# Weight splits and the residual around a LayerNorm boundary: a new order in a two-layer hybrid decoder step

## The chip, the cores and the metric

The kernel runs on one core of a Trainium2 chip. The metric is the device time of one execution in microseconds (us); a lower time is better. Times of before and after are compared on the same chip. TensorE is called PE below, VectorE DVE, ScalarE ACT, GpSimd POOL, and SyncE, which issues most loads, SP.

## The reference

One inference step for a prompt of 256 tokens and for 8 samples of 4 tokens, with shared weights: 288 columns in all. Layer 0 mixes tokens with gated linear attention (GLA), layer 1 with dilated window attention over one shared K/V. Each layer is feed-forward, mixer, feed-forward, and each sub-layer ends in a LayerNorm whose input is the scaled residual plus the gated result. Shift, scale and gate (adaLN) come from nine modulations per layer, `silu(c) @ w_ada`.

```
def post_norm(x, y, gate, g, b):
    return layer_norm(ALPHA * x + (1.0 + gate[:, None, :]) * y, g, b)

# per layer l, with sh, sc, g from silu(c) @ w_ada[l]
y = swiglu(modulate(x, sh1, sc1), w_ffn1_up[l], w_ffn1_down[l])
x = post_norm(x, 0.5 * y, g1, ln_g[l, 0], ln_b[l, 0])
h = modulate(x, sh2, sc2)
y = gla_mixer(h, ...) if l == 0 else dilated_mixer(h, ...)
x = post_norm(x, y, g2, ln_g[l, 1], ln_b[l, 1])
y = swiglu(modulate(x, sh3, sc3), w_ffn2_up[l], w_ffn2_down[l])
x = post_norm(x, 0.5 * y, g3, ln_g[l, 2], ln_b[l, 2])
```

Before layer 1 the shared K/V are projected from a modulated x. D_MODEL is 1024, D_FF 2816, all data float32.

## The kernel before

Activations lie transposed: 8 chunks of 128 features by 288 columns. A float32 product is made of three matmuls in a faster format: each operand is split into a high half and the low rest, and high x high, high x low and low x high are added in PSUM (`mm3`, lines 531 to 533).

**Weights** come through `Stream`: one list of jobs in the order of use, each cut into pieces of 512 KB. A piece is loaded by SP into one of 11 raw buffers as soon as the piece 11 places ahead of it has been released (`pump`). A piece of a projection weight is called a part. `split_part` makes its high half on ACT (line 177) and its low half on DVE (line 179), into one of 4 pairs of buffers. `take` hands out a job's halves and splits the next job's parts; `more(n)` splits n further parts ahead of time. adaLN weights are not split: they are multiplied as they are (line 450), and `fill` handles those at the head of the list. `weave` spreads adaLN jobs between the projection weights of a stage: the first `lead` weights come alone, then the others with adaLN jobs between them.

**Order.** A scheduler orders the instructions of each engine when the program is built. `pin(chain, ins)` ties an instruction behind the one pinned before it on the same chain, so pinned instructions keep the order in which the code issues them. What is not pinned may be moved far ahead, into any pause that the scheduler sees.

**A boundary** is the end of one sub-layer and the start of the next; there are five that go through `post_norm`: (0,0) after the first feed-forward, into the GLA; (0,1) after the GLA; (0,2) after the second feed-forward, into the shared K/V; (1,0) into the dilated attention's query projections (the q stage); (1,1) after it. `Post.stats` sums squares on PE, `spread` gives the inverse deviation to all partitions (line 651). Then `scaled` makes each of the 8 chunks: DVE lines 758, 763 and 764, ACT lines 760 and 765 (the high half), DVE 767 and 769 (the low half); from the fourth chunk on DVE line 668 subtracts the mean first. All these are pinned. The chunks enter `project_chunkwise` as they come: four products side by side, 12 matmuls a chunk.

Three weight parts of the next stage are split before the boundary (`more(3)`). The fourth is split behind the third chunk, by `S.more(1)` in `post_norm`. `post_norm` also returns the generator `Post.residual`: for each chunk, line 676 on DVE and line 678 on POOL write the scaled residual into `ax`, two chunks per step. In the feed-forward stages one step is run for each of the second to fifth pair of up weights. In the GLA all of it is run behind the query projection and the gates, in the q stage behind the first four products. Line 676 is not pinned.

In the q stage `rotate` (lines 1294 to 1298, on ACT, DVE and POOL) takes each product out of PSUM, and 12 query weights are woven with eight adaLN jobs, the first four weights alone. Loads of the key and value cache follow.

Of the kernel before, what the change touches and what calls it, by code (L numbers as in the profile page):

```python
# [114 lines left out]
class Stream:  # L115
# [45 lines left out]
    def part(self, low="dve"):  # L161

        x = self.parts[self.np]
        if x >= self.nd:
            return None
        self.np += 1
        i = self.pieces[x][0]
        self.split_part(self.split.setdefault(i, Weight()), self.jobs[i], self.raw.pop(x), f"{x}", low)
        self.freed.add(x)
        self.release()  # L170
        return True

    def split_part(self, w, j, src, name, low="dve"):
        cols, nk = j["nc"], src.shape[1]
        hv, lo = [self.pool.tile([P, 1024], F32R, name=q + name, tag=q, bufs=SPLIT_BUFS)[:, 0:nk * cols]
                  .rearrange("p (k c) -> p k c", c=cols) for q in ("hi", "lo")]
        self.pin("act", self.nc.scalar.activation(hv, src, AF.Copy))  # L177
        eng = self.nc.vector if low == "dve" else self.nc.gpsimd
        self.pin(low, eng.tensor_tensor(out=lo, in0=src, in1=hv.bitcast(F32), op=ALU.subtract))  # L179
        w.append([y.rearrange("p k (m c) -> p m k c", c=min(P, cols)) for y in (hv, lo)])  # L180

    def aside(self, t, j):

# [7 lines left out]
        while self.np < len(self.parts) and self.pieces[self.parts[self.np]][0] <= i and self.part():  # L191
            pass

    def more(self, n, low="dve"):

        self.pump()
        while n and self.np < len(self.parts) and self.part(low):
            n -= 1

    def fill(self, limit=None):  # L200

# [49 lines left out]
def job_list(I):  # L251
    def ada(l, mod):
        for i in range(4):
            yield dict(kind="ada", key=("ada", l, mod, i), src=ada_src(I, l, mod, i), nk=2, nc=D)

    def adas(*which):
        return [j for l, m in which for j in ada(l, m)]

    def ffn(l, n):
        up, dn = I[f"w_ffn{n}_up"][l], I[f"w_ffn{n}_down"][l]  # L260
        out = []
        for i in range(FC // 2):
            out.append(weight_job(("a", l, n, i), up, 256 * i, 256))
            out.append(weight_job(("u", l, n, i), up, FF + 256 * i, 256))
        for cb in range(4):
            for q, (k0, nk) in enumerate(((0, 8), (8, 8), (16, 6))):
                out.append(weight_job(("d", l, n, cb, q), dn, 256 * cb, 256, k0, nk))
        return out

    win = I["w_in_a"][0]  # L270
    gla = [weight_job(("wq", i), win, 256 * i, 256) for i in range(2)]
    gla += [weight_job(("glr",), win, 2048, 16)]
    gla += [weight_job(("wk", i), win, 512 + 256 * i, 256) for i in range(2)]
    gla += [weight_job(("wv", i), win, 1024 + 256 * i, 256) for i in range(4)]
    wr = [weight_job(("wr", i), win, 2064 + 256 * i, 256) for i in range(4)]
    st = []
    for i in range(4):
        src = I["state_gla"][0, 2 * i:2 * i + 2].rearrange("b h p v -> p (b h) v")
        st.append(dict(kind="r", key=("s0", i), src=src, nk=8, nc=DV))
    wo = [weight_job(("wo", i), I["w_out_a"][0], 256 * i, 256) for i in range(4)]  # L280
    kv = [weight_job(("kv", i), I["w_kv"], 256 * i, 256) for i in range(8)]
    wq = [weight_job(("q", hq, g), I["w_q_b"][0], 1024 * g + 256 * hq, 256) for hq in range(4) for g in range(3)]
    ca = []
    steps = [(g, tp) for g in (1, 2) for tp in range(2)]
    for x in range(2 * NB + 5):
        g, tp = steps[x % 4]
        k = [cache_job(I, "cache_k", g, 2 * (x // 4) + bp, tp, ("K", g, x // 4, tp, bp)) for bp in range(2) if x < 2 * NB]
        g, tp = steps[(x - 5) % 4]
        v = [cache_job(I, "cache_v", g, 2 * ((x - 5) // 4) + bp, tp, ("V", g, (x - 5) // 4, tp, bp)) for bp in range(2) if x >= 5]
        ca += k + v  # L290
    wob = [weight_job(("wob", i), I["w_out_b"][0], 256 * i, 256) for i in range(4)]
    jobs = []
    for j in range(4):
        for h in range(2):
            src = I["w_ada"][0, 4 * h * P:4 * h * P + 4 * P, 0:2 * D].rearrange("(k p) (m c) -> p k m c", p=P, m=2)
            jobs.append(dict(kind="first", key=("first", j, h), src=src[:, :, :, 256 * j:256 * j + 256], nk=4, nc=512))
    x = GAP
    jobs += weave(ffn(0, 1)[2:], adas((0, 2), (0, 3), (0, 4)), lead=2, span=28) + adas((0, 5))[2:] + adas((0, 6))[:x]
    jobs += weave(gla + wr[:2], adas((0, 6))[x:] + adas((0, 7)), lead=5) + [st[0], st[1], wr[2], st[2], st[3], wr[3]] + wo + adas((0, 8))[1:] + adas((1, 0))[:x]
    jobs += weave(ffn(0, 2), adas((1, 0))[x:] + adas((1, 1), (2, 0), (2, 1)), lead=4, span=30)  # L300
    jobs += adas((1, 2))[2:] + adas((1, 3))[:x] + kv
    jobs += weave(ffn(1, 1), adas((1, 3))[x:] + adas((1, 4)), lead=4, span=30) + adas((1, 5))[2:] + adas((1, 6))[:x]
    jobs += weave(wq, adas((1, 6))[x:] + adas((1, 7)), lead=4) + ca + wob + adas((1, 8))[2:]
    jobs += ffn(1, 2)
    return jobs

# [13 lines left out]
def body(tc, I, O, C, dbg=None):  # L320
# [236 lines left out]
    class Post:  # L557
# [112 lines left out]
        def residual(self, l, s, rstd):  # L670
            ga = self.tile("lnga", n=DC)
            bb_ = self.tile("lnba", n=DC)
            V.tensor_scalar(out=ga, in0=lng(l, s), scalar1=ALPHA, scalar2=None, op0=ALU.mult)
            V.tensor_scalar(out=bb_, in0=lnb(l, s), scalar1=ALPHA, scalar2=None, op0=ALU.mult)
            for c in range(DC):
                V.scalar_tensor_tensor(out=ax[:, c, :], in0=z[:, c, :], scalar=ga[:, c:c + 1], in1=rstd, op0=ALU.mult,  # L676
                                       op1=ALU.mult)
                G.tensor_scalar(out=ax[:, c, :], in0=ax[:, c, :], scalar1=bb_[:, c:c + 1], scalar2=None, op0=ALU.add)  # L678
                if c % 2:
                    yield  # L680
# [90 lines left out]
    def post_norm(post, l, s, nxt):  # L771
# [4 lines left out]
        S.fill()  # L776
        rstd = post.tile("lnacc")
        last, rs = None, None
        for c in range(DC):
            if c > 2:  # L780
                post.center(c)
# [5 lines left out]
                next(last, None)  # L787
            last = step
            if c == 2:
                S.more(1)  # L790
        next(last, None)

        def rest():
# [12 lines left out]
    def first_group(xh, xl):  # L806
# [39 lines left out]
        scales(0)  # L846
        for k0 in (0, 4):
            for i in range(2):
                S.split_part(w[i], jfirst[i], wfirst[i][:, k0:k0 + 4, :], f"f{i}{k0}")
            if k0 == 0:  # L850
                fold_in(0)
        for j in range(4):
# [86 lines left out]
    def gla(xh, xl, residual):  # L939
# [75 lines left out]
        qk("wq", qT, DK ** -0.5)  # L1015
        for t in range(3):
            gates(t)
        for _ in residual:
            pass
        qk("wk", kT, 1.0)  # L1020
        b = flat("bcum")
        for t in range(2):
# [135 lines left out]

        for i in range(4):
            w_ = S.take(("wv", i))  # L1160
            for m in range(2):
                p_ = bankA()
                project(p_, w_, m, xh, xl)
# [596 lines left out]
```

## Time and profile before

| | us |
|---|---|
| median of 3 runs | 1561.36 |
| lowest, highest | 1559.15, 1568.56 |
| the profiled execution, its own time | 1566.59 |
| its span in the trace | 1564.5 |

The profiled execution lies 5.2 us above the median. Its busy shares are PE 95%, DVE 59%, ACT 46%, POOL 14%. The granted clock of PE is 0.98 on average. In the rows of the profile L676 is line 676 of the kernel, "x8" is the number of instructions in a row, and brackets give the idle time of the engine just before it and what ended it. Matmuls overlap, so the distance between two starts says more than a duration. In a table of stretches the columns are the stretch, its length, the busy time of PE, PEld (weight loads), DVE, ACT and POOL with the number of instructions, the granted PE clock, the share of DMA and GB/s.

### The profile page before, as it was taken

The numbers are of one execution on the slowest core, as the hardware profiler recorded it, in microseconds if no ns is written. First come the engines' busy times: TensorE is split into PE (matmuls) and PEld (weight loads), VectorE is DVE, ScalarE is ACT, GpSimd is POOL, SyncE is SP. The second block draws the span as 40 slices with busy tenths as digits, with TensorE's granted clock in tenths as the row PEclk, the third lists the DMA queues.
The fourth block names the chain that finished last, engine by engine and source line by source line (L and its number), as shares of the span: only waits on it lengthen the run. The fifth ranks groups of instructions, "written<-read, shape, count | busy, mean of one in ns | idle before, by whom it ended". The sixth has DMA issues, their size and how long they took to land.

```text
span 1564.5 us, 31623 instructions
## 1 busy us (share of the span) xinstructions
PE 1487.1 (95%) x12706; PEld 1336.2 (85%) x12706; DVE 927.6 (59%) x2020; ACT 715.7 (46%) x1178; POOL 217.2 (14%) x312
## 2 busy tenths in 40 slices
PE   6999999999899999998999999999999989899996
PEld 4999998799778999998899999898766638899995
DVE  3644545596786444448745444675775667755455
ACT  2443434755744444346444433486543343444432
POOL 0000031201522000224100003232301002200001
PEclk8999999999999999999999999999998989999998
DMA  9977685636856767864566676767687997555520
GB/s 300 321 228 241 213 273 160 214 99 199 293 190 217 233 216 236 299 209 152 179 206 204 202 239 204 250 195 246 226 303 278 348 329 256 193 162 162 175 82 31
DMA packets 238420, 342.67 MB, mean 219 GB/s; under 512 B 12471, under 2 KB 201985, under 8 KB 238274
## 3 DMA queue, kind: packets, MB, share of 16 engines
q1 hardware_dynamic: 235810, 333.34, 64.7%
q0 software_dynamic: 2048, 7.14, 1.2%
q8 instruction: 99, 1.62, 0.4%
q14 instruction: 47, 0.39, 0.1%
q10 hardware_dynamic: 416, 0.17, 0.0%
HBM read 332.36 MB, written 8.26 MB: 218 GB/s over the span
## 4 chain that ended last, share of the span: by engine, by line
PE 83%; DVE 9%; ACT 3%; issue 2%; DMA 1%; POOL 0%; SPq 0%; DVEq 0%; ACTq 0%; POOLq 0%
PE pa L531 21%; PE pa L532 21%; PE pa L533 21%; PE pd L450 4%; PE pb L1381 4%; PE pa L1384 3%; PE pa L1381 2%; DVE lo L179 1%; PE pa L1042 1%; ACT pe L1407 1%; DVE xm L758 1%; DVE ax L676 1%; DMA xp<-in_x_prompt_dram 1%; ACT hi L177 0%; DVE lnacc L664 0%
## 5 line engine op out<-in xcount | busy, mean ns | idle before, releaser
L532 PE MATMUL pa<-xl,hi 128*128 128x288 f32 x1860 | 551.6, 298 | 6.8 <-DVE xl L769 6.8
L179 DVE TENSOR_TENSOR lo<-raw,hi 128x1024 fp32r<-128x1024 f32 x350 | 421.0, 1211 | 221.3 <-ACT hi L177 220.5
L533 PE MATMUL pa<-xh,lo 128*128 128x288 f32 x1860 | 547.6, 296 | 3.7 <-DVE lo L179 3.7
L531 PE MATMUL pa<-xh,hi 128*128 128x288 f32 x1860 | 543.5, 299 | 1.2 <-DVE lnsq L1295 0.8
L177 ACT ACTIVATE hi<-raw 128x1024 fp32r<-128x1024 f32 x350 | 358.7, 1035 | 260.6 <-PE pa L532 218.3
L532 PEld LDWEIGHTS pa<-xl,hi 128*128 128x128 f32 x1860 | 351.9, 189 | 14.0 <-DVE xl L769 9.4
L531 PEld LDWEIGHTS pa<-xh,hi 128*128 128x128 f32 x1860 | 347.9, 189 | 13.5 <-issue 10.0
L533 PEld LDWEIGHTS pa<-xh,lo 128*128 128x128 f32 x1860 | 351.7, 189 | 4.3 <-DVE lo L179 4.2
L531 PE MATMUL pa<-hh,hi 128*128 128x288 f32 x704 | 209.9, 298 | 0.0
L533 PE MATMUL pa<-hh,lo 128*128 128x288 f32 x704 | 208.1, 296 | 0.0
L532 PE MATMUL pa<-hl,hi 128*128 128x288 f32 x704 | 208.1, 296 | 0.0
L874 DVE TENSOR_TENSOR sa<-pa,sa 128x288 f32<-128x288 f32 x88 | 39.7, 454 | 179.9 <-PE pa L533 175.2
L531 PEld LDWEIGHTS pa<-hh,hi 128*128 128x128 f32 x704 | 132.6, 188 | 4.3 <-issue 2.9
L532 PEld LDWEIGHTS pa<-hl,hi 128*128 128x128 f32 x704 | 132.4, 188 | 0.2
L533 PEld LDWEIGHTS pa<-hh,lo 128*128 128x128 f32 x704 | 132.4, 188 | 0.1
L875 ACT ACTIVATE hh<-sa 128x288 fp32r<-128x288 f32 x88 | 38.7, 445 | 134.0 <-DVE sa L874 131.1
L873 ACT ACTIVATE sa<-pa 128x288 f32<-128x288 f32 x88 | 34.9, 401 | 93.6 <-PE pa L533 93.5
L450 PE MATMUL pd<-raw,cT 128*32 128x256 f32 x1008 | 73.3, 385 | 1.5 <-DMA raw<-in_w_ada_dram 1.4
L593 POOL TENSOR_TENSOR z<-z,lnpiv 128x288 f32<-128x288 f32 x6 | 4.7, 801 | 482.7 <-ACT lnpiv L588 482.7
L1384 PEld LDWEIGHTS pa<-ident,raw 128*128 128x128 f32 x448 | 49.7, 144 | 20.4 <-issue 9.4
L678 POOL TENSOR_SCALAR ax<-ax,lnba 128x288 f32<-128x288 f32 x40 | 54.9, 1376 | 71.3 <-DVE xm L764 69.4
L1384 PE MATMUL pa<-ident,raw 128*128 128x128 f32 x448 | 58.4, 282 | 5.4 <-ACT kt L1512 5.4
(380 smaller groups left out, 1761.4 us busy)
## 6 DMA issues: line engine op xcount, KB each, us to landing
raw<-in_w_ffn_up_dram SPq DMA_DIRECT2D x172, 512.0 KB, 4.8
raw<-in_w_ada_dram SPq DMA_DIRECT2D x110, 512.0 KB, 5.2
raw<-in_w_ffn_down_dram SPq DMA_DIRECT2D x80, 512.0 KB, 4.6
raw<-in_cache_k_dram SPq DMA_DIRECT2D x56, 512.0 KB, 6.7
raw<-in_cache_v_dram SPq DMA_DIRECT2D x56, 512.0 KB, 7.3
raw<-in_w_in_a_dram SPq DMA_DIRECT2D x24, 512.0 KB, 4.0
raw<-in_w_q_b_dram SPq DMA_DIRECT2D x24, 512.0 KB, 4.5
raw<-in_w_ada_dram SPq DMA_DIRECT2D x32, 256.0 KB, 5.8
```

The costliest lines, as they stand in the source:

```text
L177: self.pin("act", self.nc.scalar.activation(hv, src, AF.Copy))
L179: self.pin(low, eng.tensor_tensor(out=lo, in0=src, in1=hv.bitcast(F32), op=ALU.subtract))
L450: T.matmul(ps[32 * q:32 * q + 32, :], lhsT=cT[:, k, :], rhs=raw[kk][:, 256 * q:256 * q + 256], start=(k == 0), stop=(k == DC - 1), tile_po ...
L531: ins = [T.matmul(ps, lhsT=whi, rhs=xhi, start=first, stop=False), T.matmul(ps, lhsT=whi, rhs=xlo, start=False, stop=False), T.matmul(ps, ...
L532: T.matmul(ps, lhsT=whi, rhs=xlo, start=False, stop=False),
L533: T.matmul(ps, lhsT=wlo, rhs=xhi, start=False, stop=last)]
L678: G.tensor_scalar(out=ax[:, c, :], in0=ax[:, c, :], scalar1=bb_[:, c:c + 1], scalar2=None, op0=ALU.add)
L873: A.activation(sa, pa[:, 0:NT], AF.Silu)
L874: V.tensor_tensor(out=sa, in0=pu[:, 0:NT], in1=sa, op=ALU.mult)
L875: A.activation(hh[:, m, :], sa, AF.Copy)
L1381: pin("pe", T.matmul(*a, **k))
L1384: pin("pe", T.transpose(*a))
```

## The change

`split_part` now returns a function that makes the low half; the caller runs it. `begin` starts the next part, high half alone, and returns what is left of it. `post_norm` calls `begin` ahead of the chunks and makes the low half behind the third chunk, where the whole part was split before. Line 676 is pinned to the DVE chain, so the residual's instructions stand behind all that was pinned before them. In the GLA the residual is no longer run at once behind the gates: one step (two chunks) follows each of the four `take`s of the value weights. In the q stage the first 6 query weights come alone, and the eight adaLN jobs lie between the next five; the residual is still run behind the first four products. `more` loses a parameter that was not used.

```
     def part(self, low="dve"):
...
+        rest = self.split_part(self.split.setdefault(i, Weight()), self.jobs[i], self.raw.pop(x), f"{x}", low)
+
+        def end():
+            rest()
+            self.freed.add(x)
+            self.release()
+            return True
+
+        return end if low is None else end()
...
     def split_part(self, w, j, src, name, low="dve"):
...
         self.pin("act", self.nc.scalar.activation(hv, src, AF.Copy))
-        eng = self.nc.vector if low == "dve" else self.nc.gpsimd
-        self.pin(low, eng.tensor_tensor(out=lo, in0=src, in1=hv.bitcast(F32), op=ALU.subtract))
         w.append([y.rearrange("p k (m c) -> p m k c", c=min(P, cols)) for y in (hv, lo)])
+
+        def rest():
+            self.pin("dve", self.nc.vector.tensor_tensor(out=lo, in0=src, in1=hv.bitcast(F32), op=ALU.subtract))
+
+        return rest
...
+    def begin(self):
+
+        self.pump()
+        end = self.part(None) if self.np < len(self.parts) else None
+        return end or (lambda: None)
...
-    jobs += weave(wq, adas((1, 6))[x:] + adas((1, 7)), lead=4) + ca + wob + adas((1, 8))[2:]
+    jobs += weave(wq, adas((1, 6))[x:] + adas((1, 7)), lead=6, span=11) + ca + wob + adas((1, 8))[2:]
...
     def residual(self, l, s, rstd):
...
-                V.scalar_tensor_tensor(out=ax[:, c, :], in0=z[:, c, :], scalar=ga[:, c:c + 1], in1=rstd, op0=ALU.mult,
-                                       op1=ALU.mult)
+                pin("dve", V.scalar_tensor_tensor(out=ax[:, c, :], in0=z[:, c, :], scalar=ga[:, c:c + 1], in1=rstd,
+                                                  op0=ALU.mult, op1=ALU.mult))
...
     def post_norm(post, l, s, nxt):
...
         last, rs = None, None
+        low = S.begin()
         for c in range(DC):
...
             if c == 2:
-                S.more(1)
+                low()
...
     def gla(xh, xl, residual):
...
         for t in range(3):
             gates(t)
-        for _ in residual:
-            pass
         qk("wk", kT, 1.0)
...
         for i in range(4):
             w_ = S.take(("wv", i))
+            next(residual)
             for m in range(2):
```

More of the change, by code (lines that the diff above doesn't have):

```diff
@@ L167, in part @@
         i = self.pieces[x][0]
[L168 to L171, printed above, removed]
+        rest = self.split_part(self.split.setdefault(i, Weight()), self.jobs[i], self.raw.pop(x), f"{x}", low)
[5 more added lines that the diff above has]
+        return end if low is None else end()
     def split_part(self, w, j, src, name, low="dve"):
@@ L192, in prep, with more @@
             pass
-    def more(self, n, low="dve"):
+    def more(self, n):
         self.pump()
-        while n and self.np < len(self.parts) and self.part(low):
+        while n and self.np < len(self.parts) and self.part():
             n -= 1
+    def begin(self):
+        self.pump()
+        end = self.part(None) if self.np < len(self.parts) else None
+        return end or (lambda: None)
     def fill(self, limit=None):
@@ L848, in first_group @@
             for i in range(2):
-                S.split_part(w[i], jfirst[i], wfirst[i][:, k0:k0 + 4, :], f"f{i}{k0}")
+                S.split_part(w[i], jfirst[i], wfirst[i][:, k0:k0 + 4, :], f"f{i}{k0}")()
             if k0 == 0:
```

## The prediction

> **What bounds the kernel now.** I read the page first (busy shares), then the list of waits, then the order of time at the five places where a LayerNorm ends one sub-layer and feeds the next. TensorE (PE) is busy in nearly the whole span, so an edit gains only where PE stands still, or loses where it makes PE stand still.
>
> ```profile
> span 1564.5 us, 31623 instructions
> PE 1487.1 (95%) x12706; PEld 1336.2 (85%) x12706; DVE 927.6 (59%) x2020; ACT 715.7 (46%) x1178; POOL 217.2 (14%) x312
> PE pa L532 <- DVE xl L769: 6.8, 10, 2.2
> PE pa L532 <- DVE kl L769: 2.8, 2, 2.0
> PE pd L450 <- DMA raw<-in_w_ada_dram: 1.4, 2, 0.7
> ```
>
> The two xl/kl rows (waits: total us, times, longest) are the boundaries: PE waits there for L769, the low half of a normalized chunk from VectorE (DVE). These 9.6 us are nearly all that the boundary edits can win. The third row is adaLN weights that land late; it belongs to the q stage.
>
> **Reading one boundary.** The third one (before the shared K/V), DVE in order of time (start, duration):
>
> ```profile
> 707.96 0.19 DVE L763 TENSOR_TENSOR xm<-z,rsS 128x32 f32<-128x32 f32 x1
> 708.19 0.19 DVE L764 TENSOR_TENSOR xm<-xm,affb 128x32 f32<-128x32 f32 x1
> ...
> 709.38 0.18 DVE L763 TENSOR_TENSOR xm<-z,rsS 128x32 f32<-128x32 f32 x1
> 709.48 0.51 DVE L676 SCALAR_TENSOR_TENSOR ax<-z,lnga,lnacc 128x288 f32<-128x288 f32 x1
> 709.90 0.19 DVE L764 TENSOR_TENSOR xm<-xm,affb 128x32 f32<-128x32 f32 x1
> ...
> 710.50 0.52 DVE L676 SCALAR_TENSOR_TENSOR ax<-z,lnga,lnacc 128x288 f32<-128x288 f32 x1
> 710.93 0.48 DVE L758 SCALAR_TENSOR_TENSOR xm<-z,affs,pb 128x256 f32<-128x256 f32 x1
> ...
> 711.97 0.64 DVE L767 SCALAR_TENSOR_TENSOR kl<-xm,affb,kh 128x256 fp32r<-128x256 f32 x1
> 713.30 1.22 DVE L179 TENSOR_TENSOR lo<-raw,hi 128x1024 fp32r<-128x1024 f32 x1 [0.58 <-ACT hi L177]
> 715.95 0.48 DVE L767 SCALAR_TENSOR_TENSOR kl<-xm,affb,kh 128x256 fp32r<-128x256 f32 x1
> 716.35 0.19 DVE L769 TENSOR_TENSOR kl<-xm,kh 128x32 fp32r<-128x32 f32 x1
> 724.39 0.19 DVE L769 TENSOR_TENSOR kl<-xm,kh 128x32 fp32r<-128x32 f32 x1
> ```
>
> L763 to L764 takes 0.23 us without a residual (L676) between them and 0.52 with one: a residual in that gap costs 0.29. Elsewhere it costs its 0.43 (710.50 to 710.93). From the third chunk's L769 (716.35) to the seventh's (724.39) four chunks take 2.01 us each. The fourth weight part's low half (L179) stood idle 0.58 for its high half on ScalarE (ACT).
>
> ```profile
> 707.63 0.51 ACT L760 ACTIVATE kh<-xm,affb 128x256 fp32r<-128x256 f32 x1 [2.49 <-DVE xm L758]
> 712.77 0.40 PE L532 MATMUL pa<-kl,hi 128*128 128x288 f32 x1 [0.79 <-DVE kl L769]
> 716.59 0.61 PE L532 MATMUL pa<-kl,hi 128*128 128x288 f32 x1 [1.96 <-DVE kl L769]
> 716.00:718.00 2.00, 1.41 (x6) 1.41 (x7) 1.96 (x9) 0.74 (x2) 1.38 (x1) 0.64 0.69 225
> 718.00:720.00 2.00, 2.00 (x10) 2.00 (x10) 1.97 (x9) 0.74 (x2) 1.38 (x1) 0.51 0.00 0
> ```
>
> ACT sits idle 2.49 us just ahead of the first chunk. PE waits 0.79 and 1.96, and behind the second wait its granted clock (last number but two) falls to 0.64 and 0.51.
>
> **The change, part by part.** (1) *High half first.* The 1.0 us of ACT moves into the 2.49 us hole: nothing on the path, and the low half's 0.58 goes. If its weights or its buffer came late, the first chunk would wait up to that 1.0; its buffer's last reader is the last matmul ahead of the statistics, so I take nothing. The low half stays behind the third chunk, so its raw buffer and the next load (the SP queue) come at most some 2 us sooner.
> (2) *Residual pinned on the DVE chain.* All eight L676 of a boundary leave it, with their POOL partners L678. Here, up to the third chunk's L769: three residuals in the gap (0.29 each), one outside (0.43), the 0.16 by which L767 ran longer beside POOL (0.64 against 0.48), and the 0.58: 2.04 us. Then four more gaps: 1.16. The seventh L769 comes 3.2 us earlier, at 1.72 us a chunk, and PE behind it. What is late next is still DVE, by less. **Gain here 3.2**; at least the 2.75 of the two waits less what chunk three still has to wait (I estimate 1.3 from the same rows), so 1.5 to 3.2.
>
> [...]
>
> The others, PE rows (wait in brackets), and one of DVE:
>
> ```profile
> 278.27 0.40 PE L532 MATMUL pa<-xl,hi 128*128 128x288 f32 x1 [0.96 <-DVE xl L769]
> 470.85 0.30 DVE L471 TENSOR_TENSOR mods<-pb,bT 128x36 f32<-128x36 f32 x2 [1.10 <-PE pb L466]
> 474.58 0.40 PE L532 MATMUL pa<-xl,hi 128*128 128x288 f32 x1 [2.15 <-DVE xl L769]
> 1336.20 0.40 PE L532 MATMUL pa<-xl,hi 128*128 128x288 f32 x1 [1.96 <-DVE xl L769]
> 1344.25 0.40 PE L532 MATMUL pa<-xl,hi 128*128 128x288 f32 x1 [0.16 <-DVE xl L769]
> ```
>
> First boundary: one wait of 0.96; behind it adaLN matmuls fill PE, so no more can go: **1.0** (0 to 1.0). Second: 2.15, of which DVE's own wait for a transposed modulation (1.10) may stay, if L471 keeps its place ahead of the low half; with the high half early I expect it behind: **2.1** (1.0 to 2.1). Fifth: PE still waits for DVE at the end (1344.25), so the DVE saving counts whole: 2.04 without the 0.58 (L471 and the gate stand in that hole) and 1.16: **2.6** (1.5 to 2.6). Sum of four: 8.9.
>
> (3) *Where the residual lands.* In the three feed-forward stages it comes two chunks per step, 24 times 0.43 on an engine that is about half idle:
>
> ```profile
> 310.00:370.00 60.00, 60.00 (x530) 54.53 (x529) 55.64 (x103) 32.06 (x58) 0.38 (x1) 1.00 0.48 150
> 490.00:690.00 200.00, 200.00 (x1610) 189.78 (x1610) 91.77 (x125) 80.89 (x110) 17.18 (x18) 1.00 0.72 237
> ```
>
> The second row (span, then busy PE, PEld, DVE, ACT, POOL) is such a stage: DVE 91.77 of 200, so nothing. The first row is the gated attention's value projections, where the first boundary's eight residuals land: DVE 55.64 of 60, 4.4 us free, PE never idle. Eight times 0.43 is 3.4: between 0 (all in the free time) and 3.4, or with 0.16 each beside POOL 4.7, and one slow-clock stretch as above 6.2. Queued behind them on DVE are the decayed keys and queries that the score matmuls need. I take **+1.0**, near the free end, since 3.4 fits into 4.4 but not everywhere.
> (4) *The q stage.* Here the residual stays right behind the first projections, but is now pinned behind the next weights' low halves. Fourth boundary:
>
> ```profile
> 1006.72 1.05 PE L450 MATMUL pd<-raw,cT 128*32 128x256 f32 x10
> 1013.58 0.64 PE L450 MATMUL pd<-raw,cT 128*32 128x256 f32 x8 [0.73 <-DMA raw<-in_w_ada_dram]
> 1025.27 0.62 PE L450 MATMUL pd<-raw,cT 128*32 128x256 f32 x2
> 1058.74 1.00 PE pd L450 x16
> ...
> 1021.39 1.15 ACT L1366 ACTIVATE mb<-pe 128x1152 bf16<-128x1152 f32 x1
> 1022.44 1.99 ACT L177 ACTIVATE hi<-raw 128x1024 fp32r<-128x1024 f32 x2
> 1023.52 2.36 DVE L179 TENSOR_TENSOR lo<-raw,hi 128x1024 fp32r<-128x1024 f32 x2 [0.38 <-ACT hi L177]
> 1026.64 0.40 PE L531 MATMUL pa<-xh,hi 128*128 128x288 f32 x1 [0.76 <-DVE lnsq L1295]
> ```
>
> Now 48 adaLN matmuls (three weights, 1.0 us each) fill PE's pauses here, two behind late transfers. With the weave two weights later, four query loads pass ahead of the adaLN loads on the SP queue, so at most one of the three is there in time: the 1.4 of DMA waits goes, but about 2 us of matmuls are done later, where PE has no pause. The DVE chain saves some 3 us as above, so the low halves start near 1020.5 and end near 1022.8. If the eight residuals follow at once (3.4 us), the rotation L1295, which frees the PSUM bank that PE wants, starts at 1026.2, and PE goes on at 1026.7, as before: a cost of 2 to 3, and 1.5 more if the long pause slows the clock. If the rotation comes first, PE is back 3.2 us earlier against 3.0 of moved matmuls: -0.2. I take **+1.5**, between them (-0.2 to +4.5). The later order of loads is worth nothing else: the same two jobs end the stage, and the cache loads start behind them as before.
>
> Sum: -8.9 + 1.0 + 1.5 = **-6.4**. The profiled execution took 1566.59 us (span 1564.5 and 2.1 around it) and would take 1560.2. The median of the runs is 1561.36, 5.2 below it; the same step down gives **1555**.
>
> **Rivals.** *Forecast* (0.52): 1551 to 1559. *The fills and transfers take over* (0.22): the order on PE is fixed when the program is built, and with DVE faster it will differ; in the first two boundaries PE then stands before adaLN matmuls whose loads aren't there, as at 1013.58 now. The 3.1 of those boundaries goes and two waits of 0.7 come: 1559.5. For it: the two DMA waits of the fourth boundary. Against: no such PE wait at the first two today. In this case the change does not do what it says there.
> *Slower* (0.12): one mechanism, the pinned residual holds up DVE work that PE needs. Places: the value projections (up to 6.2) and the rotation in the q stage (up to 4.5). It decides from 8.9 on; at 10.7 the kernel takes 1563. For it: 55.64 of 60. Against: PE has other projections to do there, and waited for nothing in that stage.
> *The landing is free* (0.12): residuals fit into DVE's gaps in both places: -8.9 - 0.2, so 1552; with the slow-clock stretch also gone from other pauses, down to 1548. Nothing of these: 0.02.
>
> **Numbers.** A measurement of this kernel can tell about 1% (15.6 us) from no change; all cases lie inside. Range 1547 to 1565: from the free landing with luck in the clock to the slower rival. Faster by over 1%: 0.06; within: 0.91; slower: 0.03.
>
> **What would show it.** Right: no L676 between L763 and L764 in any boundary, the high half right behind the statistics' square root, 1.7 us from L769 to L769, and waits of PE for L769 below 4 us in all. In the gated attention, PE waits for DVE under 2 us. In the q stage the gap ahead of PE's next projection decides between my two ends. It would be wrong if PE's waits come back under other names: adaLN loads at the first two boundaries, score matmuls waiting for DVE, or a rotation behind eight residuals.

## The result and the profile after

| | median, us | runs |
|---|---|---|
| before | 1561.52 | 1559.15 to 1568.56 (18) |
| after | 1553.00 | 1549.94 to 1560.59 (18) |

The ratio is 0.9946, 95% interval 0.9936 to 0.9956: between 7 and 10 us faster. The profiled execution of after took 1551.91 us, its span 1550.1, so the two profiles differ by 14.7 us and the medians by 8.5. A profile is one execution, and part of the larger difference is that of two executions.

The page of after, and from its list of waits (total us, times, longest) what PE waits for on the lines of the change, with the line numbers of after (L769 is now L783, L676 is L690, L179 is L186, L1295 is L1309):

```profile
span 1550.1 us, 31620 instructions
PE 1477.8 (95%) x12706; PEld 1330.4 (86%) x12706; DVE 928.8 (60%) x2020; ACT 714.5 (46%) x1180; POOL 217.9 (14%) x312
PE pa L547 <- DVE lo L186: 5.4, 5, 1.9
PE pd L464 <- DMA raw<-in_w_ada_dram: 3.4, 3, 1.8
PE pa L545 <- DVE lnsq L1309: 2.7, 3, 1.1
PE pa L546 <- DVE kl L783: 1.0, 1, 1.0
PE pa L546 <- DVE xl L783: 1.0, 1, 1.0
```

Waits for a chunk's low half fell from 9.6 us to 2.0. Waits for the low half of a weight part (L186) grew from 4.2 to 5.4, those for adaLN weights from 1.4 to 3.4, and those for a rotation (L1309) from 1.9 to 2.7. The third boundary in the kernel after, in order of time:

```profile
698.84 1.04 ACT L182 ACTIVATE hi<-raw 128x1024 fp32r<-128x1024 f32 x1
...
704.50 0.18 DVE L777 TENSOR_TENSOR xm<-z,rsS 128x32 f32<-128x32 f32 x1
704.72 0.19 DVE L778 TENSOR_TENSOR xm<-xm,affb 128x32 f32<-128x32 f32 x1
...
705.23 0.18 DVE L783 TENSOR_TENSOR kl<-xm,kh 128x32 fp32r<-128x32 f32 x1
705.33 1.22 DVE L186 TENSOR_TENSOR lo<-raw,hi 128x1024 fp32r<-128x1024 f32 x1
...
708.07 0.18 DVE L783 TENSOR_TENSOR kl<-xm,kh 128x32 fp32r<-128x32 f32 x1
708.31 0.40 PE L546 MATMUL pa<-kl,hi 128*128 128x288 f32 x1 [0.98 <-DVE kl L783]
709.77 0.19 DVE L783 TENSOR_TENSOR kl<-xm,kh 128x32 fp32r<-128x32 f32 x1
711.48 0.18 DVE L783 TENSOR_TENSOR kl<-xm,kh 128x32 fp32r<-128x32 f32 x1
```

The high half runs ahead of the chunks (it starts 0.94 us before the spread at 699.78), the low half follows its neighbour without a gap, no residual stands between L777 and L778, a chunk takes 1.70 us, and of the waits of 0.79 and 1.96 one of 0.98 is left.

To see where the time went I cut both profiles at six marks that can be found in each: the first matmul of `spread` at the five boundaries, and the first score matmul (KT with z), with which the query projections of the q stage end. The stretches of before and of after (stretch, length, busy us of PE, PEld, DVE, ACT, POOL, granted clock, DMA share, GB/s):

```profile
267.68:463.00 195.32, 185.92 (x1508) 159.99 (x1509) 147.36 (x295) 112.78 (x197) 47.47 (x45) 0.97 0.61 199
463.00:706.00 243.00, 240.62 (x1985) 223.70 (x1985) 125.03 (x218) 101.70 (x148) 29.10 (x27) 1.00 0.72 235
706.00:1002.60 296.60, 288.99 (x2279) 276.88 (x2279) 168.43 (x315) 138.21 (x218) 39.63 (x41) 0.99 0.62 198
1002.60:1089.06 86.46, 84.17 (x684) 75.52 (x685) 61.48 (x147) 63.53 (x125) 28.41 (x31) 1.00 0.74 249
1089.06:1325.59 236.53, 215.46 (x2445) 152.09 (x2445) 160.48 (x582) 99.02 (x206) 34.14 (x128) 0.95 0.80 288
1325.59:1564.50 238.91, 219.60 (x1653) 214.54 (x1650) 137.04 (x254) 95.67 (x134) 15.92 (x11) 0.98 0.42 133
```

```profile
266.40:459.67 193.27, 185.45 (x1509) 159.47 (x1509) 147.59 (x296) 115.01 (x200) 46.50 (x45) 0.97 0.61 201
459.67:699.78 240.11, 240.04 (x1985) 223.79 (x1985) 124.83 (x216) 100.90 (x148) 27.97 (x27) 1.00 0.73 238
699.78:993.08 293.30, 287.77 (x2278) 275.52 (x2279) 169.75 (x315) 137.53 (x219) 39.16 (x41) 1.00 0.63 200
993.08:1083.59 90.51, 84.17 (x685) 75.60 (x685) 63.02 (x147) 61.67 (x125) 27.25 (x31) 1.00 0.69 232
1083.59:1314.18 230.59, 209.43 (x2446) 148.19 (x2445) 160.34 (x582) 99.66 (x207) 34.09 (x128) 0.99 0.82 298
1314.18:1550.10 235.92, 218.99 (x1652) 214.59 (x1650) 136.41 (x254) 94.09 (x134) 20.61 (x11) 0.97 0.43 135
```

Four stretches gained: 2.05, 2.89, 3.30 and, at the end, 2.99. The q stage (fourth row) **lost 4.05**, in these two profiles all of it PE's idle time (length less busy: 2.29, then 6.34). The fifth row, scores and cache, gained 5.94 with no line of the change in it: its granted clock was 0.95 and then 0.99.

The q stage of after, its instructions on DVE, POOL and PE in order of time (`x8` is eight in a row):

```profile
1012.53 4.30 DVE L690 SCALAR_TENSOR_TENSOR ax<-z,lnga,lnacc 128x288 f32<-128x288 f32 x8
1014.79 0.64 PE L464 MATMUL pd<-raw,cT 128*32 128x256 f32 x8 [1.04 <-DMA raw<-in_w_ada_dram]
1015.40 2.31 POOL L692 TENSOR_SCALAR ax<-ax,lnba 128x288 f32<-128x288 f32 x2
1016.75 0.81 DVE L1309 TENSOR_TENSOR lnsq<-pa,ropeq 128x288 f32<-128x288 f32 x2
1017.25 0.40 PE L545 MATMUL pa<-xh,hi 128*128 128x288 f32 x1 [0.60 <-DVE lnsq L1309]
1018.54 7.26 POOL L692 TENSOR_SCALAR ax<-ax,lnba 128x288 f32<-128x288 f32 x6
1025.77 1.57 POOL L1310 TENSOR_TENSOR xm<-xm,ropeq 128x288 f32<-128x288 f32 x2
1026.61 1.00 DVE L1312 TENSOR_TENSOR z<-lnsq,xm 128x256 f32<-128x256 f32 x1 [4.62 <-POOL xm L1310]
1028.14 0.40 PE L545 MATMUL pa<-xh,hi 128*128 128x288 f32 x1 [1.08 <-DVE lnsq L1309]
```

DVE's eight residuals stand ahead of the rotation, as forecast. Their eight partners on POOL (L692, 1.2 us each) then stand between POOL's steps of the rotations (L1310), and DVE is idle for 4.62 us until one of them gets through.

### The profile page after: what moved, and what is told of

Read it like the earlier page. It is cut to its first block, busy times and chain, and to the rows that moved or that the text cites. A ratio compares the mean times of both kernels' runs of the same rounds, so it can differ in the third digit from the quotient of the medians.

```text
span 1550.1 us, 31620 instructions
## 1 busy us (share of the span) xinstructions
PE 1477.8 (95%) x12706; PEld 1330.4 (86%) x12706; DVE 928.8 (60%) x2020; ACT 714.5 (46%) x1180; POOL 217.9 (14%) x312
## 4 chain that ended last, share of the span: by engine, by line
PE 84%; DVE 8%; ACT 3%; issue 3%; DMA 1%; POOL 1%; SPq 0%; DVEq 0%; ACTq 0%; POOLq 0%
PE pa L545 22%; PE pa L546 21%; PE pa L547 21%; PE pd L464 4%; PE pb L1395 4%; PE pa L1398 3%; PE pa L1395 2%; PE pa L1055 1%; ACT pe L1421 1%; DVE lo L186 1%; DMA raw<-in_w_ada_dram 1%; DVE xm L772 1%; ACT xm L1308 1%; DMA xp<-in_x_prompt_dram 1%; DVE lnacc L678 0%
## 5 line engine op out<-in xcount | busy, mean ns | idle before, releaser
L186 DVE TENSOR_TENSOR lo<-raw,hi 128x1024 fp32r<-128x1024 f32 x350 | 420.6, 1209 | 220.5 <-ACT hi L182 220.3
L692 POOL TENSOR_SCALAR ax<-ax,lnba 128x288 f32<-128x288 f32 x40 | 58.4, 1469 | 204.3 <-DVE ax L690 204.0
```

The costliest lines, as they stand in the source:

```text
L186: self.pin("dve", self.nc.vector.tensor_tensor(out=lo, in0=src, in1=hv.bitcast(F32), op=ALU.subtract))
```

## The experiments

The theory, called A: the gain is the residual leaving DVE's chain at four boundaries, and the q stage gives some back. Rival B: the early high half carries half of the gain. For the loss in the q stage there were two causes to tell apart: W, the later adaLN loads, and P, the pinned residual with its work on POOL.

All runs, and the stretches of their profiles (1 to 6 as in the rows above, us):

| kernel | median | before beside it | ratio, 95% interval | 1 | 2 | 3 | 4 (q) | 5 (cache) | 6 |
|---|---|---|---|---|---|---|---|---|---|
| before | | | | 195.32 | 243.00 | 296.60 | 86.46 | 236.53 | 238.91 |
| e1_weave_alone | 1562.09 | 1563.28 | 0.9996, 0.9984 to 1.0007 | 193.92 | 244.10 | 296.61 | 87.15 | 232.30 | 238.97 |
| e2_high_alone | 1556.22 | 1562.19 | 0.9954, 0.9938 to 0.9971 | 194.71 | 241.36 | 297.40 | 85.25 | 232.09 | 238.36 |
| e3_residual_alone | 1557.56 | 1562.19 | 0.9969, 0.9958 to 0.9979 | 192.43 | 241.10 | 294.23 | 92.14 | 230.72 | 237.14 |
| after | 1553.00 | 1561.52 | 0.9946, 0.9936 to 0.9956 | 193.27 | 240.11 | 293.30 | 90.51 | 230.59 | 235.92 |
| c_after_again | 1554.00 | 1562.63 | 0.9944, 0.9930 to 0.9958 | 193.07 | 240.10 | 293.32 | 91.73 | 231.08 | 235.89 |
| e4_weave_back | 1552.89 | 1562.19 | 0.9938, 0.9919 to 0.9958 | 190.80 | 240.12 | 293.32 | 90.53 | 232.11 | 235.97 |
| e5_q_unpinned | 1550.26 | 1562.19 | 0.9917, 0.9899 to 0.9934 | 192.22 | 240.11 | 293.31 | 87.13 | 232.17 | 235.75 |
| e6_q_pool_late | 1552.02 | 1563.28 | 0.9928, 0.9915 to 0.9941 | 191.82 | 240.10 | 293.30 | 88.98 | 232.06 | 235.79 |
| e7_gla_at_once | 1556.79 | 1563.28 | 0.9959, 0.9944 to 0.9975 | 193.25 | 240.37 | 293.27 | 90.29 | 230.75 | 235.88 |
| e8_gla_double | 1554.92 | 1563.28 | 0.9954, 0.9942 to 0.9967 | 193.53 | 240.11 | 293.34 | 90.29 | 235.81 | 235.93 |
| f1_q_as_before | 1549.45 | 1562.63 | 0.9923, 0.9907 to 0.9939 | 192.53 | 240.11 | 293.32 | 86.38 | 230.73 | 235.84 |
| f2_copy_later | 1548.19 | 1562.63 | 0.9903, 0.9885 to 0.9920 | 191.06 | 239.54 | 292.69 | 87.56 | 232.65 | 235.26 |
| f3_low_on_pool | 1547.24 | 1562.63 | 0.9907, 0.9892 to 0.9922 | 193.37 | 240.20 | 292.68 | 84.82 | 232.43 | 234.47 |

The intervals of the ratios are 3 to 6 us wide, too wide for single terms. Some of the columns are not: in the seven profiles from after to e8, whose code is the same there (but for one tie in e6, named below), columns 2, 3 and 6 agree within 0.3 us. These settle most of what follows. Column 1 scatters by 2.5 in the five of them that share its code, column 5 by 5.2 in all seven, and an edit of 1 us can't be read from those.

**The high half alone** (`begin` and the split of `split_part`; everything else as before; the edit is against the kernel after):

```
-                pin("dve", V.scalar_tensor_tensor(out=ax[:, c, :], ...))
+                V.scalar_tensor_tensor(out=ax[:, c, :], ...)
...
+        for _ in residual:
+            pass
         qk("wk", kT, 1.0)
...
             w_ = S.take(("wv", i))
-            next(residual)
...
-    jobs += weave(wq, ..., lead=6, span=11) + ca + wob + adas((1, 8))[2:]
+    jobs += weave(wq, ..., lead=4) + ca + wob + adas((1, 8))[2:]
```

> The kernel before with the early high half alone: residual not pinned, its loop in the gated attention and the weave of the query weights as before. Theory A (the gain is the residual leaving the VectorE chain; the early high half only saves the 0.58 us of the low half's wait, at most once per boundary, and not in the one where PE has adaLN matmuls to do): 0.5 to 2 us under the kernel before, ratio 0.9987 to 0.9997, and the residuals still stand between the two sample instructions of a chunk. Rival B (the high half ahead of the chunks carries about half of the gain): 4 to 5 us, ratio 0.997.

Its third boundary, PE's waits in order of time, and the second of them in the kernel before:

```profile
714.02 0.40 PE L546 MATMUL pa<-kl,hi 128*128 128x288 f32 x1 [1.26 <-DVE kl L783]
726.15 0.41 PE L545 MATMUL pa<-kh,hi 128*128 128x288 f32 x1 [1.19 <-DVE lnsq L1310]
```

```profile
728.73 0.40 PE L531 MATMUL pa<-kh,hi 128*128 128x288 f32 x1 [1.18 <-DVE lnsq L1295]
```

The longest wait is 1.26 instead of 1.96, and PE starts the projection that waits for the first rotation 22.05 us after spread; before it did so 22.73 after. So the early high half is worth 0.68 here, near the 0.58 that theory A gave it. At the second boundary it is worth more: one wait of 0.53 and one of 0.16 are left where one of 2.15 and one of 0.16 stood (idle time 0.77 instead of 2.38), because DVE now makes the low half ahead of L471, for which it had waited 1.10.

In columns 1 to 4 and 6 it differs from before by -0.61, -1.64, +0.80, -1.21 and -0.55, 3.2 in all. The +0.80 goes with the clock: far behind the boundary, at 760 to 764, it was 0.68 and 0.50 behind waits of 0.91 and 0.46, and PE's busy time in column 3 is 1.5 longer than in e1, which has the same two waits (0.92 and 0.47) and a clock of 1.00 behind them. Without that the sum is about 4.7 (an estimate). The median fell by 6.0, with an interval from 4.5 to 9.7: outside what A allowed, and B's 0.997 lies inside. So A was too strict. In columns 2 and 6 and at the third boundary the early high half alone is worth 2.9, the residual alone (below) 6.0 in columns 2, 3 and 6, the whole change 9.2: about a third and two thirds. The profiled execution was the slowest of the six, and what makes up the rest of the 6.0 isn't settled.

**The residual alone** (pinned, and spread in the gated attention; the edit is against the kernel before):

```
-                V.scalar_tensor_tensor(out=ax[:, c, :], ...)
+                pin("dve", V.scalar_tensor_tensor(out=ax[:, c, :], ...))
...
-        for _ in residual:
-            pass
         qk("wk", kT, 1.0)
...
             w_ = S.take(("wv", i))
+            next(residual)
```

> The kernel before with the residual pinned and spread in the gated attention; high half and weave as before. Theory A: 5 to 8 us under the kernel before, ratio 0.995 to 0.997, PE waits for the chunks' low halves 2 to 4 us in all. Rival B: about 4 us, ratio 0.9975, with the 0.58 us wait of the low half for its high half still there in each boundary and PE waiting behind it.

Ratio 0.9969, inside A's range, and its interval takes in B's 0.9975 as well. Columns 2, 3 and 6 gain 1.90, 2.37 and 1.77, and the q stage loses 5.68. The wait behind the third chunk stays 1.9 us in the third and fifth boundary, since the low half still waits for its high half, as B had it. All waits for a chunk's low half sum to 6.1, more than the 2 to 4 that I gave. In the fifth the clock falls behind it (the wait in order of time, then two stretches):

```profile
1327.72 0.40 PE L532 MATMUL pa<-xl,hi 128*128 128x288 f32 x1 [1.90 <-DVE xl L769]
```

```profile
1328.26:1330.26 2.00, 2.00 (x10) 2.00 (x10) 1.93 (x8) 0.63 (x2) 0.00 (x0) 0.50 1.06 399
1330.26:1332.26 2.00, 2.00 (x12) 2.00 (x11) 1.90 (x9) 0.90 (x3) 0.00 (x0) 0.65 0.61 244
```

High half and residual together are worth more in the last stretch (2.99) than 0.55 and 1.77: together they bring the wait to 0.98, and the slow piece is not there in the profile after. How much of the difference is the clock's isn't shown.

**The weave**, alone (this edit, to the kernel before) and taken back (the same edit undone in the kernel after):

```
-    jobs += weave(wq, adas((1, 6))[x:] + adas((1, 7)), lead=4) + ca + wob + adas((1, 8))[2:]
+    jobs += weave(wq, adas((1, 6))[x:] + adas((1, 7)), lead=6, span=11) + ca + wob + adas((1, 8))[2:]
```

> The kernel before with the adaLN jobs of the q stage two weights later, nothing else. The chunks keep their residuals, so PE has its long pause in the q stage as before (24 us from spread to the next projection), but fewer adaLN matmuls are there in time. Theory W (the weave costs what it takes out of the pause): 1 to 2.5 us slower than before, ratio 1.0007 to 1.0016. Rival (the later loads cost nothing, or the waits for adaLN weights of 1.4 us go): ratio 0.999 to 1.000.

> The kernel after with the adaLN jobs of the q stage two weights earlier again (lead of 4). In the profile after, the q stage from spread to the first scores takes 90.51 us against 86.46 before: 4.05 longer, all of it idle time of PE. Theory W (the weave causes part of it: only two of three adaLN jobs in the pause, 3.4 us of waits for their loads): 1 to 2.5 us faster than the kernel after, ratio to before 0.9930 to 0.9940, q stage 88 to 89.5 us. Rival P (the pinned residual with its eight POOL instructions causes all of it, the weave nothing or a little good): same or slower than after, ratio 0.9945 to 0.996, q stage 90.5 or more.

Alone it costs 0.69 in the q stage (87.15 against 86.46), less than W gave it, and its ratio cannot be told from 1. Taken back from the kernel after, it gives nothing there: 90.53, as P had it, though the ratio (0.9938) lies in W's range; its interval is too wide to count against the stage. Idle time does fall, from 6.34 to 3.48, but it comes in one piece. The wait, in order of time, and two stretches behind it:

```profile
1016.44 1.06 PE L464 MATMUL pd<-raw,cT 128*32 128x256 f32 x2 [3.35 <-DMA raw<-in_w_ada_dram]
```

```profile
1017.29:1019.29 2.00, 2.00 (x9) 1.86 (x9) 2.00 (x4) 1.94 (x5) 2.00 (x2) 0.50 0.67 237
1019.29:1021.29 2.00, 2.00 (x10) 2.00 (x10) 1.24 (x2) 1.25 (x4) 2.00 (x2) 0.50 0.60 156
```

PE ran at a clock of 0.50 behind that pause. With the later loads of the kernel after the pause is broken up (1.77, 1.04 and 0.59 for loads, 0.60 for the rotation) and the clock stayed at 1.00. So W, if it holds at all, holds for 0.7 us, and that is less than the q stage scatters in the four profiles that share after's code there (90.29 to 91.73).

**The q stage's residual**: not pinned there, or its POOL instructions behind later rotations, or the whole q stage as before (f1: e5 with the weave back). e6 also ties all POOL additions of the residual and POOL's step of the rotation to one chain:

```
e5, f1:
-                pin("dve", V.scalar_tensor_tensor(out=ax[:, c, :], ...))
+                x = V.scalar_tensor_tensor(out=ax[:, c, :], ...)
+                if (l, s) != (1, 0):
+                    pin("dve", x)
e6:
+    biases = deque()
...
-                G.tensor_scalar(out=ax[:, c, :], in0=ax[:, c, :], scalar1=bb_[:, c:c + 1], scalar2=None, op0=ALU.add)
+                def add(c=c):
+                    pin("pool", G.tensor_scalar(out=ax[:, c, :], in0=ax[:, c, :], scalar1=bb_[:, c:c + 1], ...))
+                if (l, s) == (1, 0):
+                    biases.append(add)
+                else:
+                    add()
...
-        G.tensor_tensor(out=sw, in0=sw, in1=tab[:, 1, :], op=ALU.mult)
+        pin("pool", G.tensor_tensor(out=sw, in0=sw, in1=tab[:, 1, :], op=ALU.mult))
...
                     rotate(p_, tab, q_out(2 * hq + m, g))
+                    if biases and hq and m:
+                        biases.popleft()()
```

> The kernel after with the residual of the q stage alone not pinned, so that its eight instructions may stand among the chunks again; the other four boundaries and the weave stay. Theory P (the eight POOL instructions behind the chunks hold up the rotations): the VectorE idle time of 4.62 us for a rotation's POOL step goes, but the chunks take 2.01 us each again; PE finishes the queries 1 to 3 us earlier, ratio to before 0.9925 to 0.994. Rival (what the chunks lose eats it up): ratio 0.9945 to 0.996.

> The kernel after with the eight POOL instructions of the q stage's residual moved behind later rotations, one behind every second; the eight VectorE instructions stay where they are. Theory P (the POOL instructions hold up the rotations): the VectorE idle time of 4.62 us goes, the wait of 1.08 us of PE behind it and one or two of the waits for low halves (0.34, 0.91) too: 1 to 2.5 us faster than the kernel after, ratio to before 0.993 to 0.994. Rival (the eight VectorE instructions ahead of the rotations are what PE waits for): same as after, 0.9945.

> The kernel after with the q stage as it was before: its residual not pinned and the weave with a lead of 4; early high half, pinned residual at the other four boundaries and the spread in the gated attention stay. If the stages add up (second to fourth stage and last as in the kernel after, q stage 85.25 us as with the early high half alone, against 90.51): 4 to 5 us faster than the kernel after, ratio to before 0.990 to 0.992. Rival (with the earlier arrival at the q stage the adaLN loads are late and PE waits there as with the weave back, 3.35 us at half clock behind it): 0.993 to 0.994, q stage 88 us or more.

> The kernel after once more, as the measure for the three beside it. Ratio 0.9936 to 0.9956 as before; where the pauses of PE are the same as in its first profile, the boundaries agree within 0.1 us, and what differs between the two profiles (the clock granted in the first and the cache stages above all) is what one profile cannot tell.

Unpinned, the stage takes 87.13 and the ratio is 0.9917, a little below P's range; with the weave back the stage takes 86.38. So of the 4.05 the pin makes up 3.4 (3.2 to 4.6 against the four profiles with after's q stage), and the 0.7 between e5 and f1 is again too small to be told from scatter. POOL's work alone, moved behind later rotations, brings 1.5 (88.98; against the second profile of after, 91.73, it is 2.75). In e6 DVE's idle time of 4.62 and PE's waits of 1.08, 0.34 and 0.91 are gone, as P had it, but PE waits 1.45 for the first rotation instead of 0.60. So POOL's block is part of the loss, not all: in e6 the eight residuals on DVE still stand ahead of the first rotation, and in e5, where they don't, the stage is another 1.85 shorter. POOL in the kernel f1, in order of time:

```profile
1009.14 1.38 POOL L694 TENSOR_SCALAR ax<-ax,lnba 128x288 f32<-128x288 f32 x1 [0.63 <-DVE ax L690]
1017.24 0.79 POOL L1312 TENSOR_TENSOR xm<-xm,ropeq 128x288 f32<-128x288 f32 x1 [4.37 <-ACT xm L1310]
```

The partners lie between the chunks (the last ends at 1012.88) and POOL is idle when the first rotation comes. The chunks are slower there, but PE has adaLN matmuls to do meanwhile: its idle time in the stage is 1.76. On one chip f1 has a median of 1549.45 and after of 1554.00; the intervals of the ratios overlap, and f1's lies between the two forecasts, but the q stage (86.38 against 91.73, without the pause of 3.35) speaks for the first. In the two profiles of after, columns 2, 3 and 6 differ by 0.03 at most, and the q stage by 1.22; in the second a wait of 2.17 stands there, with matmuls 0.24 us apart behind it instead of 0.13, in the first one of 1.77, with a clock of 1.00 throughout.

**Where the residual lands in the gated attention**: at once behind the gates, or each of its DVE instructions twice.

```
e7:
+        for _ in residual:
+            pass
         qk("wk", kT, 1.0)
...
             w_ = S.take(("wv", i))
-            next(residual)
e8:
+                for _ in range(2 if (l, s) == (0, 0) else 1):
                     pin("dve", V.scalar_tensor_tensor(out=ax[:, c, :], ...))
```

> The kernel after with the residual of the gated attention run at once behind the gates, as before, but still pinned. Theory A (its place costs nothing as long as VectorE has free time there: 58.06 of 60 us busy in the profile after): within 1 us of the kernel after, ratio 0.994 to 0.995. Rival (it needs the spread: eight in a row, 3.4 to 4.3 us on VectorE plus eight on POOL, hold up the keys' and gates' work that PE needs): 2 to 4 us slower than after, ratio 0.996 to 0.997.

> The kernel after with each of the eight VectorE residual instructions of the gated attention issued twice (same result), 0.43 to 0.54 us each, 3.4 to 4.3 us more work on an engine that has 1.94 of 60 us free in that stretch. Free landing (PE does not depend on VectorE there within some us): within 1 us of the kernel after, ratio 0.994 to 0.995. Rival (VectorE was just at its limit): PE waits for decayed keys and queries, 2 to 4 us slower, ratio 0.996 to 0.997.

The value projections of the kernel after (a stretch), and the one wait that comes when all eight run at once (order of time):

```profile
308.72:368.72 60.00, 60.00 (x537) 54.54 (x536) 58.06 (x113) 32.48 (x54) 14.75 (x9) 1.00 0.49 150
```

```profile
300.87 0.40 PE L545 MATMUL pa<-xh,hi 128*128 128x288 f32 x1 [1.81 <-DVE blk L1005]
```

Spread out, the residual fills DVE to 58.06 of 60 us and PE still waits for nothing. At once, PE waits 1.81 for the logarithm of the gates, which DVE makes; the same wait is absent in after and 0.93 in e5, where the residual is spread too. Doubled, PE has one wait in the value projections that neither profile of after has (1.17, for ACT). The first stretch takes 193.25 at once and 193.53 doubled, against 193.27 and 193.07, so neither changes it by more than its scatter. The ratios, 0.9959 and 0.9954, lie between what the two theories gave, and their intervals reach into both. That is weak evidence that the landing is free, and it doesn't show that the spread is needed.

**What bounds a boundary now**: on top of f1, ACT's copy of the inverse deviation behind the third chunk instead of the first, or the fourth part's low half on POOL.

```
f2:
-            if c == 0:
-                pin("act", A.activation(rstd, pb, AF.Copy))
-            else:
+            if c:
                 next(last, None)
...
             if c == 2:
+                pin("act", A.activation(rstd, pb, AF.Copy))
                 low()
f3:
-            self.pin("dve", self.nc.vector.tensor_tensor(out=lo, in0=src, in1=hv.bitcast(F32), op=ALU.subtract))
+            eng, chain = (self.nc.gpsimd, "pool") if low is None else (self.nc.vector, "dve")
+            self.pin(chain, eng.tensor_tensor(out=lo, in0=src, in1=hv.bitcast(F32), op=ALU.subtract))
...
-            if c == 2:
+            if c == 0:
                 low()
```

> The kernel f1_q_as_before with the copy of the inverse deviation (ACT, 0.39 us) moved from behind the first chunk to behind the third. In the profile after VectorE stands 0.59 us for it ahead of the second chunk, and PE waits 0.98 for the third chunk's low half in the third and in the fifth boundary. If that idle time is on the chain: both waits fall to about 0.4 and the kernel is 1 to 1.5 us faster than f1. Rival (the second chunk then waits for ACT or the buffer instead): no difference, waits 0.98 again.

> The kernel f1_q_as_before with the fourth part's low half on POOL, started behind the first chunk, instead of VectorE behind the third (1.22 us there). If the VectorE chain is still what PE waits for: the two waits of 0.98 go, 2 us less. Rival (POOL takes some 3 us for it and VectorE slows beside it, as L767 did with 0.64 against 0.48, and POOL also holds what follows): same as f1 or slower, a chunk's instructions 0.1 to 0.2 us longer while it runs.

f2: columns 2, 3 and 6 gain 0.57, 0.63 and 0.58, so the 0.59 was on the chain; but the wait of PE stayed (1.06), as the rival had it, since PE's first low-half matmuls start earlier as well. That step of the expectation was wrong, its sum near: 1.8 in these columns, of which the q stage gives back 1.2 in this profile. f3, third boundary, DVE and POOL in order of time:

```profile
700.98 2.41 POOL L187 TENSOR_TENSOR lo<-raw,hi 128x1024 fp32r<-128x1024 f32 x1 [17.89 <-ACT hi L182]
702.77 0.66 DVE L780 TENSOR_TENSOR xm<-z,rsS 128x32 f32<-128x32 f32 x1
704.65 0.18 DVE L780 TENSOR_TENSOR xm<-z,rsS 128x32 f32<-128x32 f32 x1
```

The waits of 0.98 go and three of 0.2 to 0.3 come; beside POOL one instruction of the first chunk takes 0.66 instead of 0.18. Columns 3 and 6 gain 0.64 and 1.37, column 2 loses 0.09. f2 and f3 have the shortest medians of all, 1548.19 and 1547.24, and both beat before and after; they can't be told apart, nor from f1 (1549.45), and the two edits were not run together.

## Why the prediction was right, and where it was not

The time was forecast as 1555 and came out at 1553.0. The mechanism at the boundaries was right; that the sum came within 2 us is in part luck. Three boundaries gave 9.2 where 7.9 was forecast, the first boundary with the landing gave about 2 where nothing was forecast, and the q stage cost 4.05 where 1.5 was forecast.

- **Second boundary**, forecast 2.1: column 2 gained 2.89 in the two profiles (3.99 from the profile with the weave alone, whose code is the same there). The idle time fell from 2.38 to 0.07, as counted. The modulation's transpose (L471) did not hold it up. Of the 3.99, 1.10 go with a slow clock in that other profile (244.10 against 243.00 in the one of before, at 1.00).
- **Third**, forecast 3.2: 3.30, with the terms as counted: chunks at 1.70 (1.72 forecast), one wait of 0.98 left (1.3 estimated). But the slow stretch behind the wait was worth next to nothing there: e1, with the same wait (1.97) and a clock of 1.00 behind it, reaches the next projection only 0.16 earlier (lines in the last section). In both profiles of after the clock was 1.00. The prediction adds 1.5 for such a stretch in its upper ends for the landing (4.7 to 6.2) and the q stage (3 to 4.5); no run shows a cost of 1.5. Between before and e1, of which one has it and the other not, the difference was 0.16 here, nothing at the fifth boundary and 1.10 at the second.
- **Fifth**, forecast 2.6: 2.99, of it 2.38 idle time (19.31, then 16.93). The 0.58 that the prediction left out here counts as well: in e2 the wait is 1.28 instead of 1.96, and column 6 is 0.55 shorter.
- **First boundary and landing**, forecast 1.0 of gain and 1.0 of cost: column 1 gained 2.05, and it scatters by 2.5 in kernels with the same code there. Over all profiles it is 193.92 to 195.32 in the three with the residual as before, and 190.80 to 193.53 in the eleven with it pinned in this stage, 2.2 less in the mean. That the landing is free, the forecast's lower bound, fits this: PE is never idle in the value projections of after.
- **The q stage**, forecast +1.5 with an upper bound of 4.5: 4.05, and 3.8 to 5.3 over the four profiles with this code. This is the step that failed. Its first half was right: the rotation follows the eight residuals, and PE goes on 24.17 us after spread against 24.04 (as forecast, as before). But the step counted only DVE's instructions of the residual. Their POOL partners, 9.6 us (2.31 and 7.26), stand between the rotations and cost what comes after that point: PE waits of 1.08 for a rotation (1028.14) and of 0.34 and 0.91 for low halves that DVE makes late (1032.17 and 1034.93). The 1.4 of waits for adaLN loads did not go either: they became 3.4, and two of three jobs were in time, not one.
- **The cache stage**, forecast 0: right by the code, since it took between 230.59 and 236.53 us with nothing changed in it. The before that I worked from had its slow end, at a clock of 0.95. Stepping the sum down by the 5.2 us between the profile and its median was therefore right.

The terms of columns 2, 3, 4 and 6 make -5.1, the medians -8.5 with an interval from 7 to 10. With the 2.2 of the first stretch the terms make -7.3, inside that interval; what is left can't be told from scatter. Of the rivals, the slower one had the right mechanism and the right place (the rotation behind the pinned residual), but not enough of it to decide; the waits for loads at the first two boundaries didn't come.

## What to carry to other kernels

When an instruction is tied to a place, follow its consumers too: the work it releases on another engine arrives there in a block, and it is that engine's next customer who waits. One profile shows where time sits, but before two profiles are subtracted, cut both at marks and see in further profiles which stretches repeat: here three of six repeat within 0.3 us and one scatters by 6. An edit that is good at four places may be left out at the fifth: leaving it out there, with the weave as before, made the stage 4 to 5 us shorter, and the others kept their gain.

## What the runs showed of the hardware

The same pause of PE was followed by a slow clock in one execution and not in another. Behind 3.35 us of waiting (e4) and 3.31 (e3) in the q stage the granted clock was 0.50 over 4 us (1017.29 to 1021.29, and 1021.40 to 1025.40) and 0.92 and 0.69 over the next 4. Waits of 1.90 to 2.15 us for a low half stand eight times in before, e1 and e3, at the second, third and fifth boundary: behind four of them the clock fell to between 0.50 and 0.65 for about 4 us, behind the other four it stayed at 1.00. before and e1 run the same code there and have the same waits (2.15, then 1.96 or 1.97, then 1.96). In before the clock fell at the third boundary alone, in e1 at the second and the fifth alone. The third boundary of e1, to be set beside the one of before in the prediction (two PE rows in order of time, and the stretch behind the first of them):

```profile
715.65 0.40 PE L532 MATMUL pa<-kl,hi 128*128 128x288 f32 x1 [1.97 <-DVE kl L769]
727.64 0.40 PE L531 MATMUL pa<-kh,hi 128*128 128x288 f32 x1 [1.03 <-DVE lnsq L1295]
```

```profile
715.65:719.65 4.00, 3.71 (x24) 3.25 (x24) 3.93 (x15) 1.48 (x4) 2.74 (x3) 1.00 0.19 67
```

What the slow clock cost went with whether PE would have waited behind it anyway. At the third boundary the second row comes 22.57 us after spread (705.07) in e1 and 22.73 in before: 0.16 for 4 us at 0.64 and 0.51. At a clock of 1.00 PE has short waits for DVE there (busy 3.71 of the 4.00 above; in the fifth boundary of before 0.16 or 0.17 behind each of four chunks), and in the slow stretch of before it has none. At the fifth the matching row comes 22.04 after spread in both. At the second, where adaLN matmuls stand in most of these pauses, column 2 is 244.10 with the slow clock and 243.00 without.

The clock also fell without any wait of PE just before it. The kernel after in the first stretch, a group in order of time and two stretches:

```profile
291.12 2.95 PE L999 MATMUL pa<-wg,ga 17*128 17x512 f32 x6
```

```profile
290.40:294.40 4.00, 4.00 (x19) 1.40 (x12) 1.74 (x5) 2.21 (x4) 0.00 (x0) 1.00 1.07 370
294.40:298.40 4.00, 4.00 (x21) 4.00 (x20) 0.69 (x1) 3.96 (x5) 0.00 (x0) 0.57 0.88 356
```

Here PE is never idle; six matmuls of the gates, with only 17 rows of weights, fill 2.95 us, and behind them the clock is 0.57. During or behind these matmuls the clock fell in ten of the fourteen profiles (lowest over 4 us: 0.50 in before, 0.57 in after, 0.50 in the second after, 0.59 in e4, 0.61 in e6) and not in e1, e3, e5 and f2. In these four PE waits 0.93 for DVE some 8 us later, and that wait is absent in after, so here too the slow clock takes up time that PE would have waited.

In f3 POOL took 2.41 us for a subtraction of 128x1024 that takes DVE 1.22, and an instruction of DVE that ran meanwhile took 0.66 instead of 0.18. For the 128x288 addition POOL took 1.2 us in the q stage of after (eight in 9.57) and 1.38 in the mean of all 40 in before, about three times the 0.43 that a residual's product took on DVE in before (710.50 to 710.93).
